# Intra-chunk scores of a gated-linear-attention mixer: seven decay levels against one product per chunk, with a guarded second pass at the program's end

## The chip, the cores and the metric

The program runs on one core of one Trainium2 chip. The metric is the time of one execution on the device in microseconds (us); three executions of the kernel before took 2157.50, 2157.58 and 2158.24 us, median 2157.58.

The engines are named as the profile names them: PE is TensorE (matmuls; PEld is its weight load, which runs beside the matmuls), DVE is VectorE, ACT is ScalarE, POOL is GpSimd, SP is SyncE, which issues nearly all transfers of this kernel.

## The reference

A trunk of two layers on 1024 tokens of width 1024, in float32. Each layer is an RMSNorm, a mixer, a residual addition, then RMSNorm, a dense SwiGLU of hidden width 2816 and a residual addition; a final RMSNorm ends it. Layer one's mixer is a convolution branch beside an mLSTM; the change doesn't touch it. Layer two's mixer is gated linear attention with 4 heads, key width 128 and value width 256:

```python
log_alpha = log_sigmoid(gl @ gate_w2 + gate_b) / 16        # one decay per token and key column
S_t = diag(alpha_t) S_{t-1} + k_t^T v_t ;   o_t = q_t S_t
# in chunks, with b the running sum of log_alpha inside a chunk, a its last value:
A[l, s] = sum_d q[l, d] k[s, d] exp(b[l, d] - b[s, d])     for s <= l, else 0
o = A v + (q exp(b)) S ;   S = exp(a) S + (k exp(a - b))^T v
```

The decay in A sits inside the sum over d. Written as (q exp(b)) times (k exp(-b)), A is one matmul, but exp(-b) grows with the decays of the whole chunk. The reference uses chunks of 64 tokens; the kernel uses chunks of 128, which gives the same o.

## The kernel before, in words

Activations are held transposed, 128 features by 512 tokens ("half" 0 or 1 of the sequence), weights are streamed. Each wide product is made of three matmuls, `mm3` (L168, L169, L170): operands are split into a high part rounded to float32r and the low rest (`split` L141; `weights` L158 load, L161 high part on ACT, L162 low part on DVE), and low times high, high times low and high times high are added in PSUM. The feed-forward blocks use a Strassen-like scheme with seven products of half-size blocks (`ffn_up`, `ffn_down`).

The order of instructions on each engine is set by a scheduler at build time from the order of the code, priorities, buffer counts and its own estimate of durations; each engine then runs its list in order and waits on semaphores. PSUM has two rings of four banks, "mm" for the wide products and "sm" for the rest.

Layer two's mixer is `mixer1`. The list ORDER1 sets its steps: p (projections of a head: q, values v, k), r (the output gate's projection), x (`head_mix`, both halves or half a or b), o (`head_out`) and k (the split of the first half's outputs for the output projection). So the wide projections of one head stand in the code beside the mixing of another, and the scheduler interleaves them on PE.

- `decays` (L771 to L795) makes for each head and half the tile `bs`: 16 times the running sum b inside each chunk of 128 tokens, for 128 key columns by 512 tokens. The matmuls are at L780, the running sums (scans) at L795.
- `head_mix`, for one head and half: L820 and L823 make qt = q exp(b). L828 to L830 make kt = k exp(a - b); L833 transposes its chunks (three in the second half, since the last chunk's state is not needed), L835 copies them to `kw`. L842 multiplies k and q per chunk without decays, and L843 keeps the diagonal in `A`.
- Then come seven levels w = 64, 32, ..., 1. At each, a chunk is cut in blocks of 2w, and pairs (l, s) with l in the upper and s in the lower half of one block get their decay relative to the block's middle, so no exponent is above 0. Per level: DVE differences (L857, L860 twice), ACT exponential (L862), DVE products with k and q (L863, L866 twice), two PE matmuls of 128 by 128 for two chunks each (L869), and a DVE copy under the level's mask into `A` (L871). The even chunks' scores land on the lower triangle's place and the odd chunks' on the other, so that one matmul serves two chunks; two transposes (L875), a copy under a mask (L876) and a POOL select (L877) then put them right.
- L887 (chunk's addition to the state), L888 (A v) and L890 (qt times the state) finish; the state is carried on DVE (L893, L895), the output is copied and squared on ACT (L898, L902). `head_out` scales it and transposes it (L917, L919).

After the mixer, `out_proj` loads the output projection's weights (L158 from `in_od_out`) and the residual's tiles (L268, from the tensor `xsp` in HBM), and `ffn_up`'s first weights (L1021, from `in_w13`, the profile's in_w) go into a pool whose memory `mixer1` held before. All of these are on SP's one queue. The kernel ends in `last_tokens`: the last products, ACT and DVE work on the last 256 tokens, and stores (L1411, L1414). The closing block (L1531) waits for all stores and brings the engines together.

Of the kernel before, what the change touches and what calls it, by code (L numbers as in the profile page):

```python
# [8 lines left out]
F32 = mybir.dt.float32  # L9
F32R = mybir.dt.float32r  # L10
U8 = mybir.dt.uint8
AF = mybir.ActivationFunctionType
# [3 lines left out]
P = 128  # L16
# [49 lines left out]
LEVELS = [64, 32, 16, 8, 4, 2, 1]  # L66

# [6 lines left out]
def trunk_kernel(ctx, tc, xT, cols, gate_b0, ev_vo0, ev_u, ev_cw, ev_out, od_v0, od_u, od_out, gate_w2, fin_row,  # L74
                 w13, w2, out, xsp, rowd, ud, zd, ad, md):
# [627 lines left out]
    def mixer1(h, cut, then):  # L703
        y = [[None, None] for _ in range(KT)]
        with tc.tile_pool(name="m1", bufs=1, reuse_waits="tile") as mp:
            unit = iter(range(30))
            masks = []
            for w in LEVELS:

                nb = P // (2 * w)  # L710
                m = mp.tile([P, nb, 2 * w], F32, tag="junk", name=f"mf{w}", bufs=1)
                POOL.memset(m, 1.0)
                for half, at in ((m[:, :, w:], 0), (m[:, :, :w], w)):

                    POOL.affine_select(out=half, in_=half, compare_op=ALU.is_ge, fill=0.0, base=-at,
                                       pattern=[[-2 * w, nb], [0, w]], channel_multiplier=1)
                    POOL.affine_select(out=half, in_=half, compare_op=ALU.is_ge, fill=0.0, base=at + w - 1,
                                       pattern=[[2 * w, nb], [0, w]], channel_multiplier=-1)
                mu = mp.tile([P, P], U8, tag=f"mk{w}", name=f"mk{w}")
                DVE.tensor_copy(mu, m.rearrange("p b x -> p (b x)"))  # L720
                masks.append(mu)
            m = mp.tile([P, P], F32, tag="junk", name="mft", bufs=1)
            POOL.memset(m, 1.0)
            POOL.affine_select(out=m, in_=m, compare_op=ALU.is_ge, fill=0.0, base=-1, pattern=[[1, P]], channel_multiplier=-1)
            above = mp.tile([P, P], U8, tag="above", name="above")
            DVE.tensor_copy(above, m)

# [37 lines left out]
            def decays(glc):  # L765

                es = []
                for half in range(2):
# [3 lines left out]
                    glr = mp.tile([P, HALF], F32R, tag="qt", name="glr", bufs=1)  # L772
# [16 lines left out]
                for half in range(2):  # L789
                    for hd in range(HEADS):  # L790
                        lf = bsum[hd][half]
                        DVE.tensor_tensor(out=lf, in0=lf, in1=es[2 * half + hd // 2][:, hd % 2, :], op=ALU.subtract)
                        for c in range(4):
                            sl = slice(c * P, (c + 1) * P)
                            DVE.tensor_tensor_scan(out=lf[:, sl], data0=one, data1=lf[:, sl], initial=0.0,  # L795
                                                   op0=ALU.mult, op1=ALU.add)

# [17 lines left out]
            def head_mix(hd, half, q, k, v, st):  # L815
                bs = bsum[hd][half]
                b3 = bs.rearrange("p (c t) -> p c t", c=4)

                qt = mp.tile([P, HALF], F32, tag="qt", name=nm("qt"), bufs=1)
                ACT.activation(qt, bs, AF.Exp, scale=1.0 / 16)  # L820
                ea = mp.tile([P, 4], F32, tag="ea", name=nm("ea"), bufs=2)
                ACT.activation(ea, b3[:, :, P - 1], AF.Exp, scale=1.0 / 16)
                DVE.tensor_tensor(out=qt, in0=qt, in1=q, op=ALU.mult)  # L823

                n = 4 - half
                kt = tmp()[:, :n * P]
                kt3 = kt.rearrange("p (c t) -> p c t", c=n)
                DVE.tensor_tensor(out=kt3, in0=b3[:, :n, P - 1:P].to_broadcast([P, n, P]), in1=b3[:, :n], op=ALU.subtract)  # L828
                ACT.activation(kt, kt, AF.Exp, scale=1.0 / 16)
                DVE.tensor_tensor(out=kt, in0=kt, in1=k[:, :n * P], op=ALU.mult)  # L830
                kb = bank("sm")[:, :n * P]
                for c in range(n):
                    PE.transpose(kb[:, c * P:(c + 1) * P], kt[:, c * P:(c + 1) * P], ident)  # L833
                kw = mp.tile([P, HALF], F32, tag="kw", name=nm("kw"), bufs=1)[:, :n * P]
                ACT.activation(kw, kb, AF.Copy)  # L835
# [38 lines left out]
                for j in range(2):  # L874
# [3 lines left out]
                                   pattern=[[0, 2], [1, P]], channel_multiplier=-1)  # L878
                og = mp.tile([P, 4, 256], F32, tag="og", name=nm("og"), bufs=OGB)
# [448 lines left out]
    def before(g):  # L1328

        hs = []  # L1330

        def done(xs, half, c0=0):
            if g == C_MIX + 8:
                for k in range(KT):
                    SP.dma_start(xsp[k, half], xs[k])
            d, work = norm_half(xs, g, half)
            hs.append(d)
            return work
        return hs, done
# [178 lines left out]
def _build(a):  # L1518
# [11 lines left out]
    args.append(nc.dram_tensor("ad", (LEAD, 2, P, HALF), F32, kind="Internal").ap())  # L1530
    with tile.TileContext(nc, schedule_with_timeline_sim=True) as tc:  # L1531
        trunk_kernel(tc, *args, md)
# [15 lines left out]
```

## Time and profile before

| | |
|---|---|
| time, median of three executions | 2157.58 us |
| span of the profiled execution | 2155.3 us |
| outside of the span (median less span) | 2.3 us |
| PE matmuls, busy | 2145.3 us of the span |
| DVE busy | 1541.7 us |
| ACT busy | 868.6 us |
| POOL busy | 22.9 us |
| layer two's mixer with its scores on PE (first L842 to last L917) | 1154.1 to 1474.7 us |

The profiled execution's own time is listed only as its span; the median of the timed executions lies 2.3 us above it, and changes are counted against the span and then carried to the median.

How to read the rows: a group of instructions is given as line, engine, operation, output and inputs by the program's names, shapes, count, then busy time in us and the mean ns of one, then the engine's idle time just before them and what ended it. A float32 matmul (not float32r) appears as two matmul records, so 112 such instructions give x224. Matmuls overlap: a new one starts before the modelled end of the last, so what a matmul takes from PE is the distance of the starts, not its own length. The granted clock of PE is 1.000 over the whole span.

### The profile page before, as it was taken

The numbers are of one execution on the slowest core, as the hardware profiler recorded it, in microseconds if no ns is written. First come the engines' busy times: TensorE is split into PE (matmuls) and PEld (weight loads), VectorE is DVE, ScalarE is ACT, GpSimd is POOL, SyncE is SP. The second block draws the span as 40 slices with busy tenths as digits, with TensorE's granted clock in tenths as the row PEclk, the third lists the DMA queues.
The fourth block names the chain that finished last, engine by engine and source line by source line (L and its number), as shares of the span: only waits on it lengthen the run. The fifth ranks groups of instructions, "written<-read, shape, count | busy, mean of one in ns | idle before, by whom it ended". The sixth has DMA issues, their size and how long they took to land.

```text
span 2155.3 us, 28752 instructions
## 1 busy us (share of the span) xinstructions
PE 2145.3 (100%) x10750; PEld 1823.8 (85%) x10750; DVE 1541.7 (72%) x2586; ACT 868.6 (40%) x1426; POOL 22.9 (1%) x56
## 2 busy tenths in 40 slices
PE   9999999999999999999999999999999999999998
PEld 8889988888888888888889989888888888888887
DVE  7555788787776666867877746587877766668687
ACT  6302337453222322444564534355522222234554
POOL 0000000000000000000020000000000000000000
PEclk9999999999999999999999999999999999999999
DMA  4233453654432336645321011155544433265344
GB/s 159 89 123 109 141 140 116 213 187 167 166 135 95 106 107 210 203 118 167 109 71 40 21 49 30 40 160 173 193 149 166 137 95 112 97 244 172 97 128 147
DMA packets 138219, 279.02 MB, mean 129 GB/s; under 512 B 22304, under 2 KB 35488, under 8 KB 138080
## 3 DMA queue, kind: packets, MB, share of 16 engines
q1 hardware_dynamic: 137808, 276.92, 39.6%
q8 instruction: 85, 1.39, 0.3%
q14 instruction: 54, 0.44, 0.1%
q10 hardware_dynamic: 272, 0.26, 0.0%
HBM read 210.51 MB, written 66.62 MB: 129 GB/s over the span
## 4 chain that ended last, share of the span: by engine, by line
PE 99%; DVE 1%; DMA 0%; ACT 0%; issue 0%; SPq 0%; DVEq 0%; ACTq 0%
PE mm L168 21%; PE mm L169 21%; PE mm L170 21%; PE sm L170 9%; PE sm L168 9%; PE sm L169 9%; PE sm L405 2%; PE sm L869 1%; PE sm L888 1%; PE sm L887 1%; PE sm L890 1%; PE sm L618 0%; PE sm L842 0%; PE sm L917 0%; PE sm L620 0%; PE sm L585 0%
## 5 line engine op out<-in xcount | busy, mean ns | idle before, releaser
L169 PE MATMUL mm<-hL,wH 128*128 128x512 f32 x1420 | 557.5, 393 | 0.0
L170 PE MATMUL mm<-hH,wH 128*128 128x512 f32 x1420 | 554.7, 391 | 0.0
L168 PE MATMUL mm<-hH,wL 128*128 128x512 f32 x1420 | 520.2, 392 | 1.3 <-DVE wL L162 1.0
L168 PEld LDWEIGHTS mm<-hH,wL 128*128 128x128 f32 x1420 | 267.0, 188 | 57.5 <-ACT hH L332 1.4
L170 PEld LDWEIGHTS mm<-hH,wH 128*128 128x128 f32 x1420 | 267.2, 188 | 55.1 <-issue 0.2
L169 PEld LDWEIGHTS mm<-hL,wH 128*128 128x128 f32 x1420 | 267.1, 188 | 54.8 <-DVE hL L333 0.5
L169 PE MATMUL sm<-hL,wH 128*128 128x512 f32 x616 | 240.1, 390 | 0.0
L170 PE MATMUL sm<-hH,wH 128*128 128x512 f32 x616 | 239.7, 389 | 0.0
L168 PE MATMUL sm<-hH,wL 128*128 128x512 f32 x616 | 209.0, 390 | 0.0
L141 ACT ACTIVATE wH<-S 128x1024 fp32r<-128x1024 f32 x88 | 93.2, 1060 | 212.4 <-PE sm L170 212.3
L141 ACT ACTIVATE wH<-q 128x512 fp32r<-128x512 f32 x143 | 90.4, 632 | 178.5 <-PE mm L170 101.1
L141 DVE TENSOR_TENSOR wL<-q,wH 128x512 fp32r<-128x512 f32 x143 | 98.6, 689 | 72.2 <-ACT wH L141 71.8
L168 PE MATMUL mm<-wH,hL 128*128 128x256 f32 (+2 forms) x512 | 145.3, 287 | 0.6 <-DVE xy L1271 0.6
L169 PE MATMUL mm<-wL,hH 128*128 128x256 f32 (+2 forms) x512 | 145.6, 286 | 0.0
L170 PE MATMUL mm<-wH,hH 128*128 128x256 f32 (+2 forms) x512 | 145.5, 286 | 0.0
L169 PEld LDWEIGHTS sm<-hL,wH 128*128 128x128 f32 x616 | 115.7, 188 | 24.7 <-issue 0.7
L168 PEld LDWEIGHTS sm<-hH,wL 128*128 128x128 f32 x616 | 115.6, 188 | 24.4 <-PE mm L170 0.5
L170 PEld LDWEIGHTS sm<-hH,wH 128*128 128x128 f32 x616 | 115.6, 188 | 24.2 <-issue 0.2
L141 DVE TENSOR_TENSOR wL<-S,wH 128x1024 fp32r<-128x1024 f32 x88 | 107.4, 1221 | 23.9 <-ACT wH L141 23.9
L1075 DVE TENSOR_TENSOR c<-sm,c 128x512 f32<-128x512 f32 x110 | 75.6, 687 | 67.6 <-PE sm L170 67.6
L161 ACT ACTIVATE wH<-raw 128x1024 fp32r<-128x1024 f32 (+2 forms) x77 | 81.4, 1057 | 96.6 <-PE mm L170 66.7
L162 DVE TENSOR_TENSOR wL<-raw,wH 128x1024 fp32r<-128x1024 f32 (+2 forms) x77 | 94.1, 1222 | 35.4 <-ACT wH L161 35.4
(332 smaller groups left out, 3688.3 us busy)
## 6 DMA issues: line engine op xcount, KB each, us to landing
raw<-in_w SPq DMA_DIRECT2D x108, 512.0 KB
mdT<-c SPq DMA_DIRECT2D x88, 256.0 KB
m<-mdT SPq DMA_DIRECT2D x88, 256.0 KB
mdB<-c SPq DMA_DIRECT2D x66, 256.0 KB
q<-in_w SPq DMA_DIRECT2D x60, 256.0 KB
m<-mdB SPq DMA_DIRECT2D x55, 256.0 KB
xsp<-xy SPq DMA_DIRECT2D x48, 256.0 KB
raw<-in_od_u SPq DMA_DIRECT2D x22, 512.0 KB
```

Source lines behind the costliest of these rows:

```text
L141: ins = ACT.activation(dst[0], src, AF.Copy), lo.tensor_tensor(out=dst[1], in0=src, in1=dst[0], op=ALU.subtract)
L161: first = ACT.activation(hi, raw, AF.Copy)
L162: cuts = lo.tensor_tensor(out=low, in0=raw, in1=hi, op=ALU.subtract)
L168: return (PE.matmul(o, lt[1], rt[0], start=start and not on, stop=False, skip_group_check=on), PE.matmul(o, lt[0], rt[1], start=False, sto ...
L169: PE.matmul(o, lt[0], rt[1], start=False, stop=False, skip_group_check=on),
L170: PE.matmul(o, lt[0], rt[0], start=False, stop=stop, skip_group_check=on))
L405: PE.matmul(o, w[:, m * P:(m + 1) * P], raw[:, e, m:m + NT], start=m == 0, stop=m == SH)
L869: PE.matmul(lb[:, j * P:(j + 1) * P], X[:, 2 * j * P:(2 * j + 1) * P], X[:, (2 * j + 1) * P:(2 * j + 2) * P], start=True, stop=True)
L887: PE.matmul(db[:, cc, :], kw[:, cs], v[:, c, :], start=True, stop=True)
L888: PE.matmul(ob[:, cc, :], A[:, cs], v[:, c, :], start=True, stop=st is None)
L890: PE.matmul(ob[:, cc, :], qt[:, cs], st, start=False, stop=True)
L1075: DVE.tensor_tensor(out=out, in0=a, in1=b, op=ALU.add)
```

## The change

It replaces the levels in the kernel's normal pass, and adds a check and a second pass:

- `mixer1` gets an argument `levels`. With False (the normal pass) no level masks are made, only one causal mask; two tiles `A0` and `A1` are cleared once at the start and reused in turn.
- In `head_mix`, k is multiplied in place by exp(-b) (ACT exponential L917 of the new file, DVE L918), kt is that times exp(a) (L919). `at_once` multiplies k exp(-b) by qt per chunk (L847, four matmuls of the same size as L842 before) and copies the causal half into `A` (L848). The seven levels, the transposes at L875 and the POOL select are not run. `qt` has two buffers.
- `decays` copies the last column of each running sum into `least` (L810, eight copies), and `bounded` takes the least of all of them: a DVE reduction (L817), a PE transpose (L819), a second reduction (L821) and a comparison with -320 (L822) into the integer tile `fits`. The sums are 16 times b, so -320 stands for exp(20).
- Layer two's input is kept in a tensor of its own, `x1`, where `xsp` served for both.
- After layer two, every engine loads `fits` into a register (L1472) and branches (L1473). If it is 0, the input of layer two is loaded again and the whole layer is redone with the levels; its code stands between the branch and the closing block.

```diff
-    def mixer1(h, cut, then):
+    def mixer1(h, cut, then, levels):
...
+            else:
...
+                causal = mp.tile([P, P], U8, tag="causal", name="causal")
+                DVE.tensor_copy(causal, m)
+                whole = [mp.tile([P, HALF], F32, tag=f"A{i}", name=f"A{i}") for i in range(AB)]
+                for t in whole:
+                    POOL.memset(t, 0.0)
+                least = mp.tile([P, HEADS, 2, 4], F32, tag="least", name="least")
...
+                        if not levels:
+                            DVE.tensor_copy(least[:, hd, half], lf.rearrange("p (c t) -> p c t", c=4)[:, :, P - 1])
+                if not levels:
+                    bounded()
+
+            def bounded():
+
+                m = mp.tile([P, 1], F32, tag="least1", name="least1")
+                DVE.tensor_reduce(out=m, in_=least.rearrange("p a b c -> p (a b c)"), axis=mybir.AxisListType.X, op=ALU.min)
+                b = bank("sm")
+                PE.transpose(b[:1, :P], m, ident)
+                n = mp.tile([1, 1], F32, tag="least2", name="least2")
+                DVE.tensor_reduce(out=n, in_=b[:1, :P], axis=mybir.AxisListType.X, op=ALU.min)
+                DVE.tensor_scalar(out=fits, in0=n, scalar1=BOUND, scalar2=None, op0=ALU.is_ge)
...
+            def at_once(hd, half, q, k):
+
+                A = whole[(2 * hd + half) % AB]
+                pb = bank("sm")
+                for c in range(4):
+                    cs = slice(c * P, (c + 1) * P)
+                    PE.matmul(pb[:, cs], k[:, cs], q[:, cs], start=True, stop=True)
+                DVE.copy_predicated(A.rearrange("p (c t) -> p c t", c=4), causal.unsqueeze(1).to_broadcast([P, 4, P]),
+                                    pb.rearrange("p (c t) -> p c t", c=4))
+                return A
+
+            def by_levels(bs, q, k):
...
+                else:
+                    e = tmp()
+                    ACT.activation(e, bs, AF.Exp, scale=-1.0 / 16)
+                    DVE.tensor_tensor(out=k, in0=e, in1=k, op=ALU.mult)
+                    DVE.tensor_tensor(out=kt3, in0=k.rearrange("p (c t) -> p c t", c=4)[:, :n],
+                                      in1=ea[:, :n].unsqueeze(2).to_broadcast([P, n, P]), op=ALU.mult)
...
+                A = by_levels(bs, q, k) if levels else at_once(hd, half, qt, k)
...
+    fits = cp.tile([1, 1], I32, tag="fits", name="fits")
     h1, done = before(C_MIX + 8)
     layer(0, mixer0, ev_out, xT, C_FFN, done)
-    layer(1, lambda cut, then: mixer1(h1, cut, then), od_out, xsp, C_FFN + 8, finish)
+    layer(1, lambda cut, then: mixer1(h1, cut, then, False), od_out, x1, C_FFN + 8, finish)
+    ok = nc.values_load(fits, min_val=0, max_val=1, skip_runtime_bounds_check_because="a comparison gives 0 or 1")
+    with tc.If(ok < 1, preferred_fallthrough_block=False):
+        h = []
+        for half in range(2):
+            xs = [xy(k, half) for k in range(KT)]
+            for k in range(KT):
+                SP.dma_start(xs[k], x1[k, half])
+            h.append(norm_half(xs, C_MIX + 8, half)[0])
+        layer(1, lambda cut, then: mixer1(h, cut, then, True), od_out, x1, C_FFN + 8, finish)
```

The scheduler makes a new order around these steps. Three places are shown; the matmul rows at L168 to L170 are L170 to L172 in the new file, mm_... is a bank of a wide product, hH/hL and wH/wL are the split halves of an activation and of a weight.

On PE, at the first `head_mix` of layer two, before:

```order
L170 MATMUL mm_10346<-wH_10315,hH_1590_8738 128x256
L168 MATMUL mm_10346<-wH_10315,hL_1594_8745 128x256
L833 MATMUL sm_10021<-ident,t_10017 128x128 x4
L842 MATMUL sm_10029<-qk_9553,qk_9830 128x128 x4
L869 MATMUL sm_10043<-t_10035 128x128 x2
L869 MATMUL sm_10055<-t_10047 128x128 x2
L169 MATMUL mm_10346<-wL_10316,hH_1593_8744 128x256
L170 MATMUL mm_10346<-wH_10315,hH_1593_8744 128x256
```

and at the same place now, up to the first matmul of the state (L936, which was L887):

```order
L170 MATMUL mm_10133<-wH_10102,hL_1597_8752 128x256
L171 MATMUL mm_10133<-wL_10103,hH_1596_8751 128x256
L923 MATMUL sm_9987<-ident,t_9982 128x128 x4
L847 MATMUL sm_9994<-qt_9977,qk_9795 128x128 x4
L172 MATMUL mm_10133<-wH_10102,hH_1596_8751 128x256
L171 MATMUL mm_10159<-wL_10103,hH_1587_8733 128x256
L172 MATMUL mm_10159<-wH_10102,hH_1587_8733 128x256
L170 MATMUL mm_10159<-wH_10102,hL_1591_8740 128x256
```

The transposes and the plain scores stay, with qt in the place of q; the pairs of L869 that followed are gone, and wide products stand there at once. Between L847 and L936 stand 18 rows of wide products of 256 columns, and 7 more before the first product with `A` (L937).

On SP's queue, in the output projection after the mixer, before (raw<-in_od_out are its weights, raw<-in_w the feed-forward's first four, xsp<-xy stores of finished tiles):

```order
L158 DMA raw_13156<-in_od_out 128x1024
L973 DMA xsp<-xy_2304_12906 128x512
L158 DMA raw_13190<-in_od_out 128x1024
L973 DMA xsp<-xy_2309_12940 128x512
L158 DMA raw_13224<-in_od_out 128x1024
L973 DMA xsp<-xy_2314_12974 128x512
L158 DMA raw_13258<-in_od_out 128x1024
L1021 DMA raw_13553<-in_w 128x1024
L1021 DMA raw_13555<-in_w 128x1024
```

and now:

```order
L160 DMA raw_12409<-in_od_out 128x1024
L1070 DMA raw_12806<-in_w 128x1024
L1070 DMA raw_12808<-in_w 128x1024
L1070 DMA raw_12878<-in_w 128x1024
L1070 DMA raw_12880<-in_w 128x1024
L270 DMA xy_2275_12585<-x 128x512
L1022 DMA xsp<-xy_2185_12159 128x512
L270 DMA xy_2280_12619<-x 128x512
L160 DMA raw_12443<-in_od_out 128x1024
```

The four loads of the feed-forward's weights stand behind the second of the second half's eight weights (raw_12409) and ahead of the third, where before they stood behind the fifth (raw_13258).

At the end of SP's list before:

```order
L1414 DMA out<-xy_3395_18471 128x2x256
L1414 DMA out<-xy_3399_18487 128x2x256
L1411 DMA out<-xy_3401_18493 128x256 x2
L1531 UNCONDITIONAL_BRANCH
```

and now:

```order
L1463 DMA out<-xy_3276_17724 128x2x256
L1463 DMA out<-xy_3280_17740 128x2x256
L1460 DMA out<-xy_3282_17746 128x256 x2
L1472 TENSOR_LOAD fits
L1473 COMPARE_AND_BRANCH
L1473 UNCONDITIONAL_BRANCH
L160 DMA raw_18157<-in_od_u 128x1024
```

The first branch decides, the second jumps over the repeated layer (whose first load is the last row) to the closing block; every engine has these three instructions at its end. The closing block followed the stores directly before.

More of the change, by code (lines that the diff above doesn't have):

```diff
@@ L707, in mixer1 @@
             masks = []
-            for w in LEVELS:
-                nb = P // (2 * w)
-                m = mp.tile([P, nb, 2 * w], F32, tag="junk", name=f"mf{w}", bufs=1)
-                POOL.memset(m, 1.0)
[L713 to L726, printed above, removed]
+            if levels:
+                for w in LEVELS:
+                    nb = P // (2 * w)
+                    m = mp.tile([P, nb, 2 * w], F32, tag="junk", name=f"mf{w}", bufs=1)
+                    POOL.memset(m, 1.0)
+                    for half, at in ((m[:, :, w:], 0), (m[:, :, :w], w)):
+                        POOL.affine_select(out=half, in_=half, compare_op=ALU.is_ge, fill=0.0, base=-at,
+                                           pattern=[[-2 * w, nb], [0, w]], channel_multiplier=1)
+                        POOL.affine_select(out=half, in_=half, compare_op=ALU.is_ge, fill=0.0, base=at + w - 1,
+                                           pattern=[[2 * w, nb], [0, w]], channel_multiplier=-1)
+                    mu = mp.tile([P, P], U8, tag=f"mk{w}", name=f"mk{w}")
+                    DVE.tensor_copy(mu, m.rearrange("p b x -> p (b x)"))
+                    masks.append(mu)
+                m = mp.tile([P, P], F32, tag="junk", name="mft", bufs=1)
+                POOL.memset(m, 1.0)
+                POOL.affine_select(out=m, in_=m, compare_op=ALU.is_ge, fill=0.0, base=-1, pattern=[[1, P]], channel_multiplier=-1)
+                above = mp.tile([P, P], U8, tag="above", name="above")
+                DVE.tensor_copy(above, m)
+            else:
+                m = mp.tile([P, P], F32, tag="junk", name="mft", bufs=1)
+                POOL.memset(m, 1.0)
+                POOL.affine_select(out=m, in_=m, compare_op=ALU.is_ge, fill=0.0, base=0, pattern=[[1, P]], channel_multiplier=-1)
+                causal = mp.tile([P, P], U8, tag="causal", name="causal")
[4 more added lines that the diff above has]
+                least = mp.tile([P, HEADS, 2, 4], F32, tag="least", name="least")
@@ L771, in decays @@
                         PE.transpose(b[:, c * P:(c + 1) * P], glc[:, half * 4 + c].rearrange("p a b -> p (a b)"), ident)
-                    glr = mp.tile([P, HALF], F32R, tag="qt", name="glr", bufs=1)
+                    glr = mp.tile([P, HALF], F32R, tag="qt", name="glr", bufs=1 if levels else 2)
                     ACT.activation(glr, b, AF.Copy)
@@ L813, in head_r @@
                         DVE.scalar_tensor_tensor(out=t, in0=e, scalar=1.0, in1=b, op0=ALU.add, op1=ALU.mult)
[L815 to L835, printed above, removed]
+            def at_once(hd, half, q, k):
[8 more added lines that the diff above has]
+            def by_levels(bs, q, k):
                 A = mp.tile([P, HALF], F32, tag="A", name=nm("A"), bufs=AB)
@@ L878, in head_mix @@
                                    pattern=[[0, 2], [1, P]], channel_multiplier=-1)
+                return A
+            def head_mix(hd, half, q, k, v, st):
+                bs = bsum[hd][half]
+                b3 = bs.rearrange("p (c t) -> p c t", c=4)
+                qt = mp.tile([P, HALF], F32, tag="qt", name=nm("qt"), bufs=1 if levels else 2)
+                ACT.activation(qt, bs, AF.Exp, scale=1.0 / 16)
+                ea = mp.tile([P, 4], F32, tag="ea", name=nm("ea"), bufs=2)
+                ACT.activation(ea, b3[:, :, P - 1], AF.Exp, scale=1.0 / 16)
+                DVE.tensor_tensor(out=qt, in0=qt, in1=q, op=ALU.mult)
+                n = 4 - half
+                kt = tmp()[:, :n * P]
+                kt3 = kt.rearrange("p (c t) -> p c t", c=n)
+                if levels:
+                    DVE.tensor_tensor(out=kt3, in0=b3[:, :n, P - 1:P].to_broadcast([P, n, P]), in1=b3[:, :n], op=ALU.subtract)
+                    ACT.activation(kt, kt, AF.Exp, scale=1.0 / 16)
+                    DVE.tensor_tensor(out=kt, in0=kt, in1=k[:, :n * P], op=ALU.mult)
+                else:
[4 more added lines that the diff above has]
+                                      in1=ea[:, :n].unsqueeze(2).to_broadcast([P, n, P]), op=ALU.mult)
+                kb = bank("sm")[:, :n * P]
+                for c in range(n):
+                    PE.transpose(kb[:, c * P:(c + 1) * P], kt[:, c * P:(c + 1) * P], ident)
+                kw = mp.tile([P, HALF], F32, tag="kw", name=nm("kw"), bufs=1)[:, :n * P]
+                ACT.activation(kw, kb, AF.Copy)
+                A = by_levels(bs, q, k) if levels else at_once(hd, half, qt, k)
                 og = mp.tile([P, 4, 256], F32, tag="og", name=nm("og"), bufs=OGB)
@@ L1334, in done @@
                 for k in range(KT):
-                    SP.dma_start(xsp[k, half], xs[k])
+                    SP.dma_start(x1[k, half], xs[k])
             d, work = norm_half(xs, g, half)
```

5 lines of the change are left out of this document (4 added, 1 removed).

## The prediction

> **What bounds the kernel now.** I read the page first (busy shares, the chain of work that ended last), then the waits of PE, then the stage that the change touches by windows.
>
> ```profile
> PE 2145.3 (100%) x10750; PEld 1823.8 (85%) x10750; DVE 1541.7 (72%) x2586; ACT 868.6 (40%) x1426; POOL 22.9 (1%) x56
> PEclk9999999999999999999999999999999999999999
> PE 99%; DVE 1%; DMA 0%; ACT 0%; issue 0%; SPq 0%; DVEq 0%; ACTq 0%
> ```
>
> The first row has PE busy for 2145.3 of 2155.3 us; the second its clock, never cut; the third says that the chain that ended last is PE at 99%. The kernel is a list of matmuls without holes. Where does PE wait at all?
>
> ```profile
> PE sm L103 <- DVE t L100: 1.5, 1, 1.5
> PE mm L168 <- DVE wL L162: 1.0, 2, 0.6
> PE mm L168 <- DVE xy L1271: 0.6, 1, 0.6
> PE sm L620 <- DVE st L626: 0.4, 2, 0.2
> PE mm L168 <- ACT hH L332: 0.3, 1, 0.3
> ```
>
> Those are all of PE's waits: 3.8 us, and none falls in the stage that the change touches. That stage, in four windows (columns: window, length, then busy time of PE, PEld, DVE, ACT, POOL, then clock, share and rate of the transfers):
>
> ```profile
> 1140.00:1240.00 100.00, 100.00 (x697) 93.48 (x696) 70.75 (x210) 46.41 (x90) 1.03 (x2) 1.00 0.10 33
> 1240.00:1340.00 100.00, 100.00 (x586) 88.82 (x585) 54.69 (x144) 38.27 (x78) 1.23 (x3) 1.00 0.14 43
> 1340.00:1440.00 100.00, 100.00 (x513) 85.16 (x512) 72.72 (x182) 52.46 (x96) 0.82 (x2) 1.00 0.25 75
> 1440.00:1476.00 36.00, 36.00 (x170) 30.15 (x169) 22.98 (x34) 15.56 (x26) 0.41 (x1) 1.00 0.46 155
> ```
>
> PE is busy for all 336 us, although DVE has its heavy level work there (221 us) and ACT 153. So this stage is worth what its matmuls are worth: each one taken out shortens the program by its place on PE, and DVE, ACT or POOL work taken out is worth nothing while PE stays full.
>
> **The change part by part.** *The matmuls that go.* These rows group them (line, names, shapes, count, busy, mean ns):
>
> ```profile
> L869 PE MATMUL sm<-t 128*128 128x128 f32 x224 | 32.7, 274 | 0.0
> L875 PE MATMUL sm<-ident,A 128*128 128x128 f32 x16 | 3.0, 272 | 0.0
> ```
>
> 4 heads by 2 halves by 7 levels by 2 are 112 matmuls, two records each, hence x224; they stand in 56 pairs of four records. The busy column counts a record to its modelled end, past the start of the next. What a pair takes from PE is read from the starts around it, first between products of 256 columns, then of 512:
>
> ```profile
> 1156.96 0.28 PE L169 MATMUL mm<-wL,hH 128*128 128x256 f32 x1
> 1157.08 0.28 PE L170 MATMUL mm<-wH,hH 128*128 128x256 f32 x1
> 1157.20 0.61 PE L869 MATMUL sm<-t 128*128 128x128 f32 x4
> 1157.57 0.36 PE L168 MATMUL mm<-wH,hL 128*128 128x256 f32 x1
> 1157.77 0.28 PE L169 MATMUL mm<-wL,hH 128*128 128x256 f32 x1
> ```
>
> ```profile
> 1195.14 0.39 PE L170 MATMUL mm<-hH,wH 128*128 128x512 f32 x1
> 1195.36 0.39 PE L168 MATMUL mm<-hH,wL 128*128 128x512 f32 x1
> 1195.59 0.60 PE L869 MATMUL sm<-t 128*128 128x128 f32 x4
> 1195.95 0.48 PE L169 MATMUL mm<-hL,wH 128*128 128x512 f32 x1
> 1196.27 0.40 PE L170 MATMUL mm<-hH,wH 128*128 128x512 f32 x1
> ```
>
> In the first, 1157.08 to 1157.77 is 0.69 us and holds two wide products at 0.12 (the step 1156.96 to 1157.08) and the pair: 0.45 us. In the second, 1195.36 to 1196.27 is 0.91, less two at 0.227: 0.46. So 56 times 0.455 = 25.5 us go, not the 32.7 of the busy column. The 16 records at L875 are transposes; eight of another line in one run give their step:
>
> ```profile
> 1474.09 0.88 PE sm L917 x8
> ```
>
> 0.11 us each, 16 make 1.8. Sum off PE: 27.3 us. The scores themselves (L842, now L847 with qt) and the transposes, state and output products stay one for one. Added is the transpose in `bounded`, 0.11. Net 27.2.
>
> *DVE, ACT, POOL work that goes or comes.* Of DVE's part of the levels the largest groups are these:
>
> ```profile
> L860 DVE TENSOR_TENSOR t<-bs 128x128 f32<-128x128 f32 x112 | 27.4, 283 | 0.0
> L866 DVE TENSOR_TENSOR t<-t,qk 128x128 f32<-128x128 f32 x112 | 27.3, 282 | 0.0
> L857 DVE TENSOR_TENSOR t<-bs 128x256 f32<-128x256 f32 x56 | 23.4, 417 | 7.2 <-PE sm L833 6.8 <-PE sm L869 0.2
> L863 DVE TENSOR_TENSOR t<-t,qk 128x256 f32<-128x256 f32 x56 | 23.3, 416 | 4.0 <-ACT t L862 3.6
> ```
>
> 101 us go with them, and ACT's 56 exponentials, seven masks and POOL's selects; per half one exponential and a masked copy come, and `least` once. On the time: 0, since all of it lies beside a full PE before and after.
>
> *New waits in the stage.* A now hangs on one step: scores, masked copy of 128 by 512, product with v. The nearest rows, the first of which goes too:
>
> ```profile
> L871 DVE COPY_PREDICATED A<-mk,sm 128x256 f32<-128x256 uint8 x56 | 24.7, 441 | 1.3 <-PE sm L869 1.1
> L843 DVE TENSOR_TENSOR A<-sm,ident 128x512 f32<-128x512 f32 x8 | 5.5, 685 | 0.3
> ```
>
> 0.44 us at half the size, 0.69 for the same size without a mask: I take 0.8, at most 0.9. PE has 18 and 7 products of 256 columns and a state product between scores and first use at the place shown (25 times 0.12 + 0.43 = 3.4 us). Cover 3.4 against some 1.1 with the signal: 0. Had DVE a weight split and a state update in front, it would be 1.1 + 1.2 + 0.5, still below. Without that cover it would cost about 1 us in each of eight halves.
>
> `bounded`'s transpose is queued on PE between wide products and waits for the last running sum; behind it in PE's list stands everything else.
>
> ```profile
> 1123.47 0.91 PE sm L780 x4
> 1139.92 1.36 DVE L795 TENSOR_TENSOR_SCAN bs<-one,bs 128x128 f32<-128x128 f32 x4
> 1105.13 0.21 DVE L758 COPY glc<-mm 128x48 f32<-128x48 f32 x1 [0.17 <-ACT v L756]
> ```
>
> In the new order 88 products of 512 columns stand between the last decay matmul and it: 1124.4 + 88 times 0.227 = 1144.4 in the old clock. The sums ended at 1141.3; eight copies and a reduction at about 0.2 (the last row, the nearest small DVE step) end near 1143.1. It fits by about 1 us; a weight split (1.2 us) in between would use that up. 0, up to 1.5.
>
> *SP's queue.* Three weights of the output projection are now behind four loads of 0.5 MB (raw<-in_w). Before:
>
> ```profile
> 1473.94 1.88 SPq L1021 DMA_DIRECT2D raw<-in_w  x4
> 1474.00:1480.00 6.00, 6.00 (x32) 5.12 (x31) 3.31 (x6) 3.18 (x4) 0.00 (x0) 1.00 0.88 328
> ```
>
> At 328 GB/s four take 6.4 us, the weight behind them 1.6, its split on ACT and DVE 2.3: 10.3 us after the loads may start, which is when the last transposes of the mixer are done. The first product with that weight stands 104 wide rows later, 23.6 us. 0; the 13 us left would have to go first.
>
> *The end.* After its last store SP loads a register, compares, waits for the stores as before, and jumps over the repeated layer.
>
> ```profile
> 2151.45 0.82 SPq L1411 DMA_DIRECT2D out<-xy  x2
> q8 instruction: 85, 1.39, 0.3%
> span 2155.3 us, 28752 instructions
> ```
>
> No row shows a register load or a jump. From the last issue (2152.3) to the end are 3.0 us, the stores' flight and the closing; the load and compare lie beside that flight. The jump lies behind it. Code comes in 85 packets of 16 KB (1.39 MB), each 0.3% of 16 engines' span over 85 = 1.2 us in its engine. From below 0 (the target already there); from above two blocks, each with its transfer and as long a way as the store's 3.0: 8.4. I take one block with half of that way, 1.2 + 1.5 = 2.7, nearest to the packet's row.
>
> [...]
>
> *Sum.* 2155.3 - 27.3 + 0.1 + 2.7 = 2130.8 us of span; the median of the timed runs stands 2.3 above this span, so 2133.1, and with 0.4 for small new waits of the kind listed above (before, 3.8 us in 2155 of a list ordered in the same way) **2133.5 us**.
>
> **The rivals.**
>
> *A wait takes the matmuls' place* (masked copy late, `bounded` late, weights late). For it: the covers of 1 us at `bounded` and 3.4 at the scores are short, and the order rests on guessed durations. Against it: the list before, with five dependent steps more per half, left no wait in this mixer, and DVE loses most of its work. Price: 8 halves at about 1 us plus 1.5, at most 9.5: 2134.5 to 2143.
>
> *The end is dear*: two blocks in turn, 8.4 instead of 2.7: 2139.2. For it: the target is cold on every engine; against it: the other engines jump while SP waits for its stores.
>
> *The busy column is the price after all*: 32.7 + 3.0 go instead of 27.3, 2125.1. Against it: the starts of single records, above.
>
> *The second pass runs*: slower. Its place is the branch; it decides where the least 16-fold sum falls below -320. Layer two begins here:
>
> ```profile
> 1071.37 1.12 ACT wH L161
> ```
>
> It takes 2155.3 - 1071.4 = 1084 us with the levels, which the redone layer has again: 2133 + 1084 = 3217. I worked the sums out from the reference's own inputs: over 8 chunks and 512 columns they run from -245 to -29, mean -104. -320 is far, so only a fault in the check would bring it, such as the register being read before `fits` is written.
>
> *The change does nothing for the time*: PE would have to be idle where the pairs stood, and some 20 us of new waits be there; no row points to that.
>
> **How the numbers follow.** Forecast (PE stays full, end 0 to 5 us, waits up to 2): 2130.4 to 2137, 0.77. A wait in the mixer beyond that: 0.10. Dear end: 0.06. Busy column: 0.03. No change: 0.01. Second pass: 0.03. The range reaches below to 2129 (end at nothing, pairs at the 0.46 of the second fence and a little more) and above to 2140, into the two rivals of waits and end. About 0.2% (4.3 us) is what a measurement of this kernel can tell from no change. Faster by more: 0.77 + 0.10 + 0.06 + 0.03 = 0.96; within it 0.01; slower 0.03.
>
> **What would show it right or wrong.** Right: no line of pairs on PE, PE still at 100% in the mixer's windows, its last transposes some 27 us earlier (1474.7 to about 1447.5), `bounded`'s transpose with no idle time before it, DVE's busy time down by over 100 us without any further gain, and the span's end 2 to 4 us later behind the last store than 3.0. Wrong: PE waits at the product with A or at the transpose (first rival); a gap of over 6 us between last store and end (second); matmuls of the levels behind the branch (second pass); a mixer shorter by 35 us (busy column).

## The result and the profile after

The changed kernel takes 2133.86 us (median of four executions, 2132.78 to 2135.95) beside 2157.54 us for the kernel before (four executions, 2156.08 to 2158.24). The ratio is 0.9892 with a 95% interval of 0.9878 to 0.9906, so 23.7 us or 1.1% are gone. The profiled execution took 2133.76 us, with a span of 2132.0 us.

The page of the changed kernel, its busy times, PE's clock and the chain that ended last:

```profile
PE 2117.0 (99%) x10511; PEld 1795.9 (84%) x10511; DVE 1437.3 (67%) x2190; ACT 835.6 (39%) x1368; POOL 2.9 (0%) x15
PEclk9999999999999999999999999999999999999999
PE 97%; DVE 1%; ACT 1%; DMA 1%; issue 0%; SPq 0%; DVEq 0%; ACTq 0%
```

239 matmul records are gone from PE (224 of the levels, 16 of the transposes, one came) and 104 us of DVE's work. The kernel is still a list of matmuls without holes. PE's waits in the changed kernel (total, times, longest):

```profile
PE sm L105 <- DVE t L102: 1.5, 1, 1.5
PE mm L170 <- DVE wL L164: 1.2, 2, 0.6
PE mm L170 <- ACT hH L334: 0.9, 1, 0.9
PE mm L170 <- DVE xy L1320: 0.6, 1, 0.6
PE sm L622 <- DVE st L628: 0.4, 2, 0.2
PE mm L171 <- DVE hL L335: 0.2, 1, 0.2
```

They sum to 4.8 us beside 3.8, and again none lies in the mixer. The stage in windows, with the columns as before:

```profile
1140.00:1240.00 100.00, 100.00 (x661) 92.42 (x660) 34.66 (x57) 43.71 (x95) 0.00 (x0) 1.00 0.11 32
1240.00:1340.00 100.00, 100.00 (x555) 87.80 (x554) 29.19 (x40) 32.01 (x63) 0.00 (x0) 1.00 0.15 48
1340.00:1440.00 100.00, 100.00 (x471) 83.77 (x470) 49.39 (x70) 43.57 (x72) 0.00 (x0) 1.00 0.37 125
```

PE is full as before, and DVE has 113 us of work in these 300 us where it had 198.

Where the time left is read best between marks that both kernels pass with the same work behind them. The last matmul of the decays (L780 before, L792 now) starts at 1124.0 us in both. The transposes of the last tokens (L1368 before, L1417 now) start 27.5 us apart. First before, then after (first and last start are the two times):

```profile
L780 PE MATMUL sm<-glr,gw x8: 389/389/389, 1105.1 to 1124.0; 128*128 128x512 f32 x8
L1368 PE MATMUL sm<-ident,xy x16: 271/273/273, 2122.4 to 2133.6; 128*128 128x128 f32 x16
```

```profile
L792 PE MATMUL sm<-glr,gw x8: 389/389/398, 1105.1 to 1124.0; 128*128 128x512 f32 x8
L1417 PE MATMUL sm<-ident,xy x16: 270/272/273, 2094.9 to 2106.1; 128*128 128x128 f32 x16
```

2122.4 less 2094.9 is 27.5 us won between layer two's decays and the last tokens. The span is only 23.3 us shorter, so 4.2 us are given back behind that. They lie behind the last store. SP's issue of the last two stores, after:

```profile
2123.97 0.88 SPq L1460 DMA_DIRECT2D out<-xy  x2
```

It ends at 2124.85, and the span at 2132.0: 7.2 us, where it was 3.1 before (2152.27 to 2155.3). SP's own instructions in that stretch, by line (the two times are the first and the last start):

```profile
L1472 SPq TENSOR_LOAD <-fits x1: 882/882/882, 2124.9 to 2124.9; - x1
L1473 SPq EVENT_SEMAPHORE  x8: 17/17/17, 2126.0 to 2127.9; - x8
L1473 SPq COMPARE_BRANCH  x2: 43/46/49, 2125.9 to 2128.0; - x2
L1591 SPq EVENT_SEMAPHORE  x10: 17/28/28, 2130.7 to 2132.0; - x10
```

The register load takes 0.88 us, the eight waits for the stores last until 2127.9, the second branch runs at 2128.0 and is over in some 0.05 us, and nothing happens on SP until 2130.7. These 2.7 us belong to no instruction: they are the way from the jump to its target. SP doesn't wait for another engine there, since all of them have reached the closing block (L1591) by 2128.2:

```profile
L1473 POOLq COMPARE_BRANCH  x2: 38/42/45, 1145.5 to 1145.7; - x2
L1591 POOLq DRAIN  x3: 34/82/118, 1146.1 to 2131.8; - x3
L1591 PEldq DRAIN  x2: 8/40/73, 2126.0 to 2131.6; - x2
L1591 DVEq DRAIN  x2: 10/34/57, 2127.9 to 2131.6; - x2
L1591 ACTq DRAIN  x2: 8/44/80, 2128.2 to 2131.5; - x2
```

The only transfers from 2128.0 to 2130.7 are three packets of code:

```profile
q14 instruction: 3, 0.02, 3.3%
```

From 2120 us to its end the changed kernel fetches eight packets of code; the kernel before fetches one from 2140 us to its end at 2155.3. The rest of the 4.1 is in the last store, which is seen as landed 2.9 us behind its issue (2.1 in the kernel without the branch, so 0.8 more), and in a second round of the eight waits in the closing block (some 0.6 with the other waits and the branch).

### The profile page after: what moved, and what is told of

Read it like the earlier page. It is cut to its first block, busy times and chain, and to the rows that moved or that the text cites. A ratio compares the mean times of both kernels' runs of the same rounds, so it can differ in the third digit from the quotient of the medians.

```text
span 2132.0 us, 27718 instructions
## 1 busy us (share of the span) xinstructions
PE 2117.0 (99%) x10511; PEld 1795.9 (84%) x10511; DVE 1437.3 (67%) x2190; ACT 835.6 (39%) x1368; POOL 2.9 (0%) x15
## 4 chain that ended last, share of the span: by engine, by line
PE 97%; DVE 1%; ACT 1%; DMA 1%; issue 0%; SPq 0%; DVEq 0%; ACTq 0%
PE mm L170 21%; PE mm L171 21%; PE mm L172 21%; PE sm L172 10%; PE sm L170 10%; PE sm L171 10%; PE sm L407 2%; PE sm L937 1%; PE sm L936 1%; PE sm L939 1%; DMA wb<-rowd 0%; PE sm L847 0%; PE sm L966 0%; PE sm L620 0%; PE sm L587 0%; PE sm L622 0%
## 5 line engine op out<-in xcount | busy, mean ns | idle before, releaser
L172 PE MATMUL mm<-hH,wH 128*128 128x512 f32 x1420 | 553.7, 390 | 0.0
L170 PE MATMUL mm<-hH,wL 128*128 128x512 f32 x1420 | 518.0, 391 | 2.1 <-DVE wL L164 1.2
L170 PEld LDWEIGHTS mm<-hH,wL 128*128 128x128 f32 x1420 | 266.5, 188 | 58.8 <-ACT hH L334 1.8
L172 PEld LDWEIGHTS mm<-hH,wH 128*128 128x128 f32 x1420 | 266.7, 188 | 55.5 <-issue 0.2
L172 PE MATMUL sm<-hH,wH 128*128 128x512 f32 x616 | 239.7, 389 | 0.0
L170 PE MATMUL sm<-hH,wL 128*128 128x512 f32 x616 | 209.0, 390 | 0.0
L170 PE MATMUL mm<-wH,hL 128*128 128x256 f32 (+2 forms) x512 | 146.4, 289 | 0.6 <-DVE xy L1320 0.6
L172 PE MATMUL mm<-wH,hH 128*128 128x256 f32 (+2 forms) x512 | 146.4, 287 | 0.0
L163 ACT ACTIVATE wH<-raw 128x1024 fp32r<-128x1024 f32 (+2 forms) x77 | 81.6, 1060 | 147.1 <-PE mm L172 115.2
L170 PEld LDWEIGHTS sm<-hH,wL 128*128 128x128 f32 x616 | 115.6, 188 | 24.4 <-PE mm L172 0.5
L172 PEld LDWEIGHTS sm<-hH,wH 128*128 128x128 f32 x616 | 115.6, 188 | 24.3 <-issue 0.2
```

The costliest lines, as they stand in the source:

```text
L163: first = ACT.activation(hi, raw, AF.Copy)
L170: return (PE.matmul(o, lt[1], rt[0], start=start and not on, stop=False, skip_group_check=on), PE.matmul(o, lt[0], rt[1], start=False, sto ...
L172: PE.matmul(o, lt[0], rt[0], start=False, stop=stop, skip_group_check=on))
```

## Experiments

The theory after this result: PE's places are the whole gain, and the end gives back about 4 us, nearly all because the jump's target is far away. Its rivals: the relief of DVE has a share in the gain; the end costs what a branch costs, wherever it goes; the time goes with the new order of the list and not with the matmuls.

**The changed kernel without the branch.** The bound is still computed, and nothing reads it.

```diff
-    ok = nc.values_load(fits, min_val=0, max_val=1, skip_runtime_bounds_check_because="a comparison gives 0 or 1")
-    with tc.If(ok < 1, preferred_fallthrough_block=False):
...
-        layer(1, lambda cut, then: mixer1(h, cut, then, True), od_out, x1, C_FFN + 8, finish)
```

> The bound is still worked out, but the register loads, the branch and the second pass are left out. Theory (the matmuls give 27.5 us, the end with its branch takes 4.1 back): PE's list is that of the changed kernel, so only the end moves; from the last store's issue to the span's end 3.1 us as before the change, not 7.2; span 2127.9, time about 2129.7. Rival (the stores land later for another reason, and the branch is hidden beside them): the end stays near 7 us, time 2133.9.

Measured 2128.90 us (2128.41 to 2129.68), ratio 0.9874 (0.9859 to 0.9889), span 2126.7. From the last issue to the end are 3.1 us as in the kernel before. Of the 5.3 us of span that it is below the changed kernel, 4.1 are the end. The other 1.2 are there before the change begins: its last decay matmul starts at 1122.8 instead of 1124.0, and layer one's last matmul at L622 already at 362.7 instead of 363.9. In the kernels here, all with the same layer one, that decay matmul starts between 1122.8 and 1124.5.

**The repeated layer directly behind the branch.** Now the normal pass meets the far jump first, and waits for its stores after it.

```diff
-    with tc.If(ok < 1, preferred_fallthrough_block=False):
+    with tc.If(ok < 1, preferred_fallthrough_block=True):
```

> The same branch, but the repeated layer stands directly behind it, so the jump over it is the conditional one, which SP meets before it waits for its stores. Theory (2.7 of the 4.1 us are the fetch of code at the jump's target, exposed because it lies behind the wait): the fetch now lies beside the stores' flight of 2.9 us together with the register load of 0.9, so 0.7 to 1 us of it stay; span 2130.0 to 2130.5, time about 2132. Rival (the price is in the loads, compares and the second round of semaphore waits): nothing moves, time 2133.9.

Measured 2131.75 us (2131.45 to 2132.87), ratio 0.9887 (0.9872 to 0.9903), span 2130.0. The end behind the last issue is 5.2 us. SP's rows at the branch in this kernel:

```profile
L1472 SPq TENSOR_LOAD <-fits x1: 620/620/620, 2124.9 to 2124.9; - x1
L1473 SPq EVENT_SEMAPHORE  x8: 17/17/17, 2128.1 to 2128.7; - x8
L1473 SPq COMPARE_BRANCH  x1: 50/50/50, 2125.6 to 2125.6; - x1
```

The jump still takes 2.5 us (2125.6 to 2128.1), but the stores fly meanwhile, and the eight waits behind it pass one after the other without a stop. So the jump is a price by itself, and part of it goes if it lies beside the stores. How much is better counted from the start of the last two stores' issue, which itself took longer here (1.35 us for 0.88):

```profile
2123.46 1.35 SPq L1460 DMA_DIRECT2D out<-xy  x2
```

From there to the end are 6.6 us, 8.1 in the changed kernel and 3.9 in the kernel before: the turned branch takes back 1.5 of the 4.2 us. The other half microsecond of the 2.0 by which the spans differ is there before the change begins (last decay matmul at 1123.4).

**A small body behind the branch.** In place of the repeated layer stand eight loads that repair nothing: the guard of this kernel is empty.

```diff
-        h = []
...
-        layer(1, lambda cut, then: mixer1(h, cut, then, True), od_out, x1, C_FFN + 8, finish)
+        t = xy(0, 0)
+        for k in range(KT):
+            SP.dma_start(t[:, :256], out[k, 1, :, 256:])
```

> The branch stays where it is, but in place of the repeated layer only eight loads stand in it, so the jump's target is some dozens of instructions away. (The guard would not repair anything.) Theory (the jump costs a fetch because its target is far): the 2.7 us go, loads, compares and double waits stay; from the last store's issue to the end 4.3 to 4.6 us, span about 2129.3, time 2131.1. Rival (any taken branch costs this): 7.2 us, time 2133.9.

Measured 2130.21 us (2129.66 to 2130.67), ratio 0.9880 (0.9864 to 0.9895), span 2128.1. SP's rows at the branch:

```profile
L1472 SPq TENSOR_LOAD <-fits x1: 817/817/817, 2123.9 to 2123.9; - x1
L1473 SPq EVENT_SEMAPHORE  x8: 17/17/17, 2124.9 to 2126.1; - x8
L1473 SPq COMPARE_BRANCH  x2: 38/46/53, 2124.8 to 2126.2; - x2
L1586 SPq EVENT_SEMAPHORE  x10: 17/28/28, 2126.4 to 2128.0; - x10
```

The same branch over a short body is followed by the closing block (L1586) at 2126.35, 0.15 us behind it, and the last store is seen 2.1 us behind its issue; the end is 4.2 us instead of 7.2. It is thus the distance of the target and not the branch that takes 2.7 us. POOL shows the same inside the changed kernel: the trace of the second pass (below) has some 60 instructions of its in the repeated layer and some 740 of SP's, and its jump, in the rows further up, takes 0.4 us (1145.7 to 1146.1). The later landing goes with the far jumps: counted from the start of its issue, the last store is seen 3.2 to 3.3 us later in the kernels where the other engines jump far while it flies, the one with the turned branch included, and 2.4 us later in the others. Why, no run shows.

**The changed kernel with PE's places given back.** 112 matmuls of the levels' size are put in, into banks that nothing reads; no level work on DVE or ACT.

```diff
                                     pb.rearrange("p (c t) -> p c t", c=4))
+                for _ in LEVELS:
+                    lb = bank("sm")[:, :2 * P]
+                    for j in range(2):
+                        PE.matmul(lb[:, j * P:(j + 1) * P], k[:, 2 * j * P:(2 * j + 1) * P], q[:, (2 * j + 1) * P:(2 * j + 2) * P],
+                                  start=True, stop=True)
                 return A
```

> The changed kernel with the levels' 112 matmuls put back on PE, into a bank that nobody reads, and none of the levels' DVE and ACT work. Theory (PE's places alone are the gain): 56 pairs of 0.455 us come back, 25.5; span 2157.5, time 2159.4, above the kernel before. Rival (the relief of DVE and ACT is part of the gain): clearly less than 25 comes back, 2150 or below.

Measured 2158.07 us (2157.49 to 2159.53), ratio 1.0008 (0.9999 to 1.0017), span 2157.5: the whole gain is gone, with DVE and ACT as light as in the changed kernel. The transposes of the last tokens now:

```profile
L1422 PE MATMUL sm<-ident,xy x16: 270/272/273, 2120.3 to 2131.5; 128*128 128x128 f32 x16
```

2120.3 less 2094.9 is 25.4 us, of which 0.5 lie ahead of the change (its last decay matmul starts at 1124.5 instead of 1124.0). So the 56 pairs take 24.9 us, near the 25.5 of the starts and not the 32.7 of the busy column.

**The changed kernel once more, on another chip**, with no edit, and **the repeated layer directly behind the branch once more**, beside it:

> The changed kernel itself, to stand beside the next one on the same chip. Theory and rival alike: about 23.5 us below the kernel before.

> The kernel with the repeated layer directly behind the branch, beside the changed kernel on one chip. Theory (part of the fetch of code is covered by the stores' flight): 2 us below the changed kernel. Rival (the difference seen before was one between chips): the same as the changed kernel.

Measured 2134.13 us (2133.73 to 2135.59), ratio 0.9899 (0.9884 to 0.9915), and 2131.91 us (2131.55 to 2132.92), ratio 0.9886 (0.9871 to 0.9901). The difference of 2.2 us agrees with the 2.1 of the first pair. Of it the ends account for 1.5, as in the first pair (8.1 us less 6.6 from the start of the last issue); the rest is less than what executions of one kernel differ by. The difference is smaller than what the ratios' intervals tell apart, though no single execution of the one lies among the other's on this chip. With the branch turned round, the kernel with its guard is the fastest of those here that do the whole work and keep the check.

**The kernel before without the levels' matmuls.** The other half of the question: PE's places are taken out, and DVE and ACT keep all of the levels. The masked copy reads the products' tile in place of the scores, so the scores are not the reference's.

```diff
-                    lb = bank("sm")[:, :2 * P]
-                    for j in range(2):
-                        PE.matmul(lb[:, j * P:(j + 1) * P], X[:, 2 * j * P:(2 * j + 1) * P], X[:, (2 * j + 1) * P:(2 * j + 2) * P],
-                                  start=True, stop=True)
                     DVE.copy_predicated(even, masks[li].unsqueeze(1).to_broadcast([P, 2, P]),
-                                        lb.rearrange("p (j t) -> p j t", j=2))
+                                        X[:, :2 * P].rearrange("p (j t) -> p j t", j=2))
```

> The kernel before with the levels' 112 matmuls left out and all of their DVE and ACT work kept (the masked copies read the level's own operand instead, so the scores are not the reference's). Theory (PE's places are the gain, DVE and ACT lie beside a full PE): 56 times 0.455 = 25.5 us below the kernel before, at 2131 on a chip where that takes 2156.5, with no new wait of PE. Rival (the DVE chain of the levels would stop PE as soon as there are fewer matmuls beside it): less than 20 us gained, and PE waits for DVE in the mixer.

Measured 2138.66 us (2137.72 to 2140.26), ratio 0.9919 (0.9905 to 0.9932): 17.5 us gained and not 25.5. Here the prediction's "DVE work is worth nothing" has its limit. PE's waits of this kernel:

```profile
PE mm L168 <- DVE wL L162: 4.9, 2, 4.2
PE sm L103 <- DVE t L100: 1.5, 1, 1.5
PE mm L168 <- ACT hH L332: 1.1, 1, 1.1
PE mm L168 <- DVE xy L813: 0.7, 1, 0.7
```

The 4.2 us stand where the output projection begins. PE in that stretch (in brackets the idle time before a row and what ended it):

```profile
1414.22 0.39 PE L169 MATMUL mm<-hL,wH 128*128 128x512 f32 x1
1414.45 0.39 PE L170 MATMUL mm<-hH,wH 128*128 128x512 f32 x1
1419.06 0.79 PE L168 MATMUL mm<-hH,wL 128*128 128x512 f32 x1 [4.22 <-DVE wL L162]
1419.65 0.63 PE L169 MATMUL mm<-hL,wH 128*128 128x512 f32 x1
1420.08 0.63 PE L170 MATMUL mm<-hH,wH 128*128 128x512 f32 x1
...
1422.08 0.39 PE L169 MATMUL mm<-hL,wH 128*128 128x512 f32 x1
```

And the windows around it (PE, PEld, DVE, ACT, POOL, clock, transfers):

```profile
1400.00:1414.00 14.00, 14.00 (x78) 11.95 (x76) 13.97 (x35) 5.77 (x11) 0.00 (x0) 1.00 0.32 96
1414.00:1420.00 6.00, 1.78 (x6) 1.21 (x5) 6.00 (x14) 4.28 (x6) 0.00 (x0) 0.87 0.47 171
1420.00:1425.00 5.00, 5.00 (x19) 4.00 (x18) 3.70 (x11) 0.63 (x1) 0.00 (x0) 0.81 0.65 208
```

DVE is full from 1400 to 1420: the split of the projection's weight stands in its list behind the last head's levels. Starts are 0.227 us apart before the gap; behind it seven products take 3.0 us (1419.06 to 1422.08) instead of 1.6; the granted clock is 0.81 in that window (0.50 from 1418.5 to 1421.9). Idle 4.4 and slow restart 1.4 make 5.8 us at this one place, and the wait at L813, also in the mixer, 0.7. The 0.8 that PE waits longer than before at L332 lie at the start of layer one, which the edit doesn't touch. From the last decay matmul to the last tokens 18.5 us are gained, so 7 of the 25.5 are missing there, and 6.5 of them are found.

**A part of the levels' DVE work, and three heads' of it.** Two more edits of that kernel tell whether the amount at this one place is the cause. The first also leaves out the levels' products on DVE (L863 and L866, 51 of the levels' 126 us there):

```diff
-                    E2.tensor_tensor(out=lo3[:, :, :w], in0=lo3[:, :, :w], in1=k3[:, :, :w], op=ALU.mult)
-                    for e in range(2):
-                        up = hi5[:, :, 1 - e, :, w:]
-                        DVE.tensor_tensor(out=up, in0=up, in1=q5[:, :, e, :, w:], op=ALU.mult)
```

> The kernel before without the 112 level matmuls (as in levels_no_mm) and also without the 168 DVE products of the levels (L863, L866), so DVE keeps only half of the level work; the scores are not the reference's. levels_no_mm gained 17.5 us instead of 25.5, and its trace shows PE waiting 4.2 us at the output projection for a DVE weight split that stands behind level work of the last head. If DVE's level work in front of that split is the cause, half of it leaves the split in time: PE's wait falls below 1 us, and the time is 2130 to 2133 us beside 2156.3 for the kernel before. If the wait comes from something else (weight buffers that come free late, the new order as such), it stays: 2137 to 2140.

The second keeps the levels' work for three heads and drops it for the last:

```diff
-                for li, w in enumerate(LEVELS):
+                for li, w in enumerate(LEVELS if hd < 3 else []):
```

> The kernel before without the 112 level matmuls, with all DVE and ACT level work kept for the first three heads and none for the last head, whose levels stood beside the start of the output projection; the scores are not the reference's. If it is the amount of level work at that one place that delays the split, the wait goes as in lv_half: 2130 to 2133 us, although three quarters of the level work are still there. If DVE is too slow over the whole mixer once PE has 25 us less to do, waits appear inside the first three heads: 2134 to 2139.

Measured 2130.76 us (2130.22 to 2131.32), ratio 0.9883 (0.9866 to 0.9899), and 2130.61 us (2130.24 to 2130.77), ratio 0.9881 (0.9867 to 0.9896), beside 2156.33 for the kernel before: 25.6 and 25.7 us, the full price of the pairs. In the second, that wait and its window:

```profile
PE mm L168 <- DVE wL L162: 0.6, 1, 0.6
```

```profile
1414.00:1420.00 6.00, 6.00 (x29) 5.10 (x28) 2.79 (x4) 2.46 (x7) 0.00 (x0) 1.00 0.43 135
```

PE is full again, although three quarters of the levels' DVE work are still in the mixer. It was the last head's levels in front of one weight split, and not DVE's load as a whole. As the scheduler makes a new order for each of these kernels, the runs don't tell the amount of this work apart from its place in DVE's list.

**The second pass taken.** The bound is set so that the inputs fail it.

```diff
-BOUND = -320.0
+BOUND = -200.0
```

> The bound raised to -200, so that the least sum of -245 fails it and layer two is redone with the levels. Theory: the changed kernel plus one layer two with its levels, 1084 us, plus a fetch of code at the start of the layer on every engine and the first weights' way of some 10 us: 3220 to 3235. Rival (the branch never tests what it says): 2133.

Measured 3237.76 us (3236.21 and 3239.31, two executions), ratio 1.5015 (1.4988 to 1.5043). The repeated layer costs 1104 us more than the 2134.13 of the same chip, where the prediction took the 1084 of layer two from the trace of before. The stretch of the second pass:

```profile
2132.00:3220.00 1088.00, 1069.06 (x5324) 908.81 (x5325) 778.53 (x1365) 463.14 (x745) 15.68 (x30) 0.99 0.35 117
```

That is a little above the 3220 to 3235 us that were expected. PE is idle for 18.9 of these 1088 us, nearly all of it at the start, where it waits for the norm of an input that must first come back from HBM. From the layer's first weight (L161 at 1071.4 before, L163 at 2131.7 now) to the end are 1105.9 us, 22.0 more than before, and 20.7 of them lie ahead of the layer's last decay matmul (2205.1 now). Part of that is the clock: it is granted at 0.50 until 2157.8, and at 0.99 on the mean of the stretch above.

## Why the prediction was right, point by point

The forecast was 2133.5 us, the result 2133.86, inside the range. The mechanism was the one given. That the sum came within 0.4 us is partly luck: the end was 1.4 us too small, and against it stood 0.5 us in the term outside of the span, 0.4 for small new waits of which none is left between the marks, and 0.3 at PE's places.

- *The matmuls that go.* Predicted 27.2 us net, measured 27.5 between the marks. That the pairs are worth their distance of starts (25.5) and not the busy column (32.7) is shown by the kernel with the places given back (24.9) and by the two without them (25.6 and 25.7).
- *DVE, ACT and POOL at nothing.* Right for the changed kernel: it gains no more than PE's places, and DVE's relief alone (places given back) gains nothing. But the reason "beside a full PE before and after" holds after only because the DVE work went too. With all of it kept, the same removal from PE is worth 17.5 us. The relief is worth 7 to 8 us there, 5.8 of them at one place, and two fifths of it would have been enough. The prediction did not ask what a shorter list on PE does to DVE's old cover.
- *New waits in the stage at nothing.* Right. The masked copy takes 0.74 us (0.8 taken), and no wait stands at the product with `A`. At `bounded` the estimate was a margin of about 1 us. DVE's rows and PE's transpose (L819) there in the changed kernel:

```profile
1140.11 1.22 DVE L164 TENSOR_TENSOR wL<-raw,wH 128x1024 fp32r<-128x1024 f32 x1
...
1141.91 0.16 DVE L810 COPY least<-bs 128x4 f32<-128x4 f32 x1
1142.11 0.18 DVE L817 TENSOR_REDUCE least<-least 128x1 f32<-128x32 f32 x1
...
1144.16 0.27 PE L819 MATMUL sm<-ident,least 128*1 128x128 f32 x1
1144.47 0.28 DVE L821 TENSOR_REDUCE least<-sm 1x1 f32<-1x128 f32 x1 [1.57 <-PE sm L819]
```

  A weight split did come in between (1140.11), as feared, but the last running sum had ended at 1140.1, 1.1 us earlier than in the list before. So the reduction ends at 1142.3, 1.6 us before PE loads its result for the transpose (1143.9), and it is DVE that waits for PE there, not the reverse.
- *SP's queue at nothing.* Right: no wait of PE's list above lies between 1090 and 1460 us, so no weight of the output projection came late.
- *The end.* 2.7 us were taken for the jump, the load and compare beside the stores' flight. The jump measured 2.7 and the load lay beside the flight, but the end is 4.1 us longer: the last store seen 0.8 us later and the second round of waits were not in the sum. The term was sized 1.4 us too small. That the jump took the very 2.7 us is luck too: no run shows it to be made of one packet (1.2) and half of a store's way (1.5), and in the same kernel DVE's jump took 3.5 us (2124.4 to 2127.9). The reason for the size, code far away, is shown by the runs: 2.7 and 2.5 us over the long body, 0.15 over the short one. The trace has 0.04 and 0.05 us for SP's two branch instructions themselves.
- *Outside of the span.* 2.3 us were taken as the median of before less its profiled span. In the four executions of the changed kernel the time lies 1.7 to 1.8 above the span of the same execution. The 2.3 held half a microsecond of scatter, which hid part of the end's miss.
- *What would show it.* DVE's busy time fell by 104 us without any further gain, and the transpose in `bounded` has no idle time before it, as said. The end is 4.1 us longer, where "2 to 4" was said. Two signs were wrong. From the last store's issue to the end are 7.2 us, and a gap of over 6 was named as the sign of the dear end. That limit was set too low: the "2 to 4" beside it allowed 7.0, and two blocks in turn would have made 11.4. The other: the last transposes of the mixer were to start near 1447.5, and they start at 1432.0.

```profile
L966 PE MATMUL sm<-ident,og x64: 270/272/275, 1202.5 to 1432.0; 128*128 128x128 f32 x64
```

  That is 42.7 us earlier and not 27. Read by itself it would have spoken for the rival "busy column" (35 us). Since PE is full in both kernels, mixer steps must have moved ahead of wide products which now stand behind them, so the mark no longer has the same work in front of it; the mark at the last tokens, which has, gives 27.5.
- *The rivals.* No wait took the matmuls' place, but the kernel without the levels' matmuls shows it was near: there waits and a slow restart took 7 to 8 of 25.5 us. A dear end did not come: 4.1 us were added and not 8.4. The second pass did not run, and its price is 1104 us.

## What to carry to other kernels

Where PE is full, price a removed matmul by the distance of the starts around it (25.5 us for the 56 pairs here, where three experiments gave 24.9 to 25.7 and the busy column had 32.7), and check the gain at marks that have the same work in front of them in both kernels, since a scheduler moves the others. When PE's list gets shorter, look again at each split or copy that another engine makes in time only because PE was busy: the work removed beside the matmuls may be what keeps the gain (7 to 8 of 25.5 us here). A rarely taken second pass costs less if the jump over it is met while the last stores fly (2.7 us here instead of 4.2), so put the long body directly behind the branch and the wait for the stores after it.

## What the runs showed of the hardware that was not expected

- A jump over the long body took 2.7 us on SP (2.5 with the branch turned round), 2.7 on ACT, 3.5 on DVE and 0.4 on POOL, which has little code there. Over eight loads it took SP 0.15 us. The branch instruction itself took 0.04 to 0.05 us on SP in both.
- Loading one word from SBUF into an engine's register took 0.5 to 0.9 us (SP 0.88, 0.82 and 0.62 in three kernels).
- The last store was seen 3.2 to 3.3 us behind the start of its issue where the engines jumped far meanwhile, and 2.4 us where they jumped near or not at all.
- After 4.2 us of idle time, PE's products of 512 columns stood 0.43 us apart instead of 0.227 for some 2.5 us, with a granted clock of 0.50 from 1418.5 to 1421.9. So this wait on PE cost a third more than its own length (5.8 us beside 4.4).
